# The down-projection of a hybrid encoder block by seven products of halved matrices, and forms remade product by product

## The chip, the core and the metric

The kernel runs on one core of one Trainium2 chip. The metric is the time of one execution in microseconds on that core. The engines are TensorE (PE, with PEld for its weight loads), VectorE (DVE), ScalarE (ACT), GpSimd (POOL) and the sync engine (SP), which here only issues DMAs. Matrices are float32; each is split into a high part in fp32r and the rest, and a product is three matmuls (high x high, high x low, low x high).

## The reference

One layer of a bidirectional encoder block, 2048 rows of width 1024: attention and a recurrent group, an output projection onto the residual (its result is called x1 in the kernel), then a gated MLP with a short convolution, and a final norm. The change lies in the last three lines:

```python
h = rms_norm(x, norm2_g[l])
u = depthwise_conv(h @ w_up[l], up_conv_w[l], up_conv_b[l], 1, 1)   # w_up: 1024 x 6144
gate, val = jnp.split(u, 2, axis=-1)
x = x + (jax.nn.gelu(gate) * val) @ w_down[l]                       # w_down: 3072 x 1024
return rms_norm(x, final_g)
```

## The kernel before

The attention, the recurrence and the output projection come first and are not touched. The MLP begins at about 1413 us of the span.

**Up-projection by steps.** The width of the gated product is cut into 24 tiles f of 128, the rows into two halves of 1024. Step i is one f for one half: steps 0 to 23 are f = 0 to 23 with the second half, steps 24 to 47 f = 23 to 0 with the first. The product of a step is a 2x2 product of halved matrices: on the weight's side a gate tile and a value tile, each in two halves of the inner width; on the side of the rows four blocks of 512 rows by 512. It is formed by seven products instead of eight, from sums of the halves. Such a sum, split into its high and low part, is called a form here. `a_forms` makes the seven forms of a step's weights (tiles `fa`) a step ahead: the sums on POOL (`a_srcs`, L1298 to L1306), the splits on ACT (L141) and DVE (L146). The forms of the rows (tiles `fb`, 7 products by 4 pieces of 128 of the inner width) stay over a half's 24 steps; there is one buffer for each.

`step` (from line 1530) issues seven products of 4 x 3 = 12 matmuls each (L1388). The products have four banks of PSUM: products 0 to 3 have banks 0 to 3, and products 4, 5 and 6 go on adding into banks 0, 3 and 2. So before product 5 (the sixth) TensorE waits until DVE has read bank 3 with the add behind product 4 (L1469, `y<-pu,y`). Behind each product the loop calls three generators in this order: `before`, which finishes the previous step (adds, convolution taps at L1503 and L1512, GELU at L1525, gate times value at L1527, store to `g_d`); `nxt`, a form of the next step's weights; and `side`, work that is spread over many steps. Each engine runs its instructions in the order in which they are issued. At a step's start `load_w(i + 2)` issues the loads of the weights of two steps later on SP. Of the three buffers `raw` the second is free only when a split of the current step has read it, so SP's queue stands until then.

**The change between halves.** Forms of the first half of the rows need sums of blocks. `sums_ahead`, the side work of steps 2 to 17, loads four blocks a unit, makes four sums in DVE (L1259, L1261, L1578, L1580) and stores them to `t_d`; there are four units. In step 23 the products are issued tile by tile of the inner width instead (`step_by_tile`, seven banks), and behind each piece its form is remade (`form`, through a ring of nine tiles `rg` that `load_ring` fills).

**Down-projection.** It runs over four blocks of 512 rows, 24 tiles f each, and for each f over 4 row tiles and two halves of the output width, three matmuls each (L1706), 2304 in all, that add up in eight banks over f. A tile f of `w_down` and of `g_d` is loaded and split some units ahead. At a block's end the rows of x1 are added, normed and stored (L1716 to L1730).

Of the kernel before, what the change touches and what calls it, by code (L numbers as in the profile page):

```python
# [20 lines left out]
D = 1024  # L21
KT = 8
# [61 lines left out]
def block_kernel(ctx, tc, x, g1, wqkv, wxy, qkg, rope, cw, cb, wg, bg, lam, w_out, g2,  # L84
# [22 lines left out]
    t_d = [dram.tile([128, 4, 512], F32, name=f"t_d{k}") for k in range(4)]  # L107
    g_d = [dram.tile([128, S], F32, name=f"g_d{f}") for f in range(FT)]
# [55 lines left out]
    with tc.manual_schedule():  # L164
# [1061 lines left out]
        steps = [(1, f) for f in range(FT)] + [(0, f) for f in range(FT - 1, -1, -1)]  # L1226
        raws, fa, fb, got = {}, {}, {}, {}
# [340 lines left out]
        def sums_ahead():  # L1568

            for k in range(4):  # L1570
                yield from load_b(0, k)
                for _ in range(10):
                    yield
                yield from b_sums(0, k, DVE)
                b11, b12, b21, b22 = got.pop((0, k))
                t3 = t3s.pop((0, k))
                yield
                DVE.tensor_tensor(out=b11, in0=t3, in1=b11, op=ALU.add)  # L1578
                yield
                DVE.tensor_tensor(out=b21, in0=b21, in1=b11, op=ALU.subtract)  # L1580
                for _ in range(3):
                    yield
                for n, t in enumerate((t3, b12, b11, b21)):
                    dma(out=t_d[k][:, n, :], in_=t)
                for _ in range(6):
                    yield

        ring, todo = [], []

        def load_ring():  # L1590
# [4 lines left out]
            k, j = n // 7, ORDER[n % 7]  # L1595
            t = tbp[n % 9 // 5].tile([128, 512], F32, tag=("t3", "b0", "b1", "b2", "b3", "b0", "b1", "b2", "b3")[n % 9],
                                     name="rg")
            src = {0: h2_d[0][:, k, :], 4: h2_d[0][:, k + 4, :], 5: h2_d[1][:, k + 4, :]}
            for m, jj in enumerate((2, 3, 1, 6)):
                src[jj] = t_d[k][:, m, :]  # L1600
            dma(out=t, in_=src[j])
            ring.append(t)

        def step_by_tile(i, before, made, change=False):

            for k in range(made, 4):
# [3 lines left out]
                for n, j in enumerate(by_tile(i, k)):  # L1610
# [5 lines left out]
                    if change:  # L1616
                        form(j, k, ring[7 * k + n])
                        load_ring()
            run(out)
            return conv(i)  # L1620

# [6 lines left out]
        side = sums_ahead()  # L1628
        for i in range(1, len(steps)):
            if i == FT - 2:  # L1630
                run(side)
                for _ in range(9):
                    load_ring()
            if i == FT - 1:
                left = chain(wait(2), step_by_tile(i, left, 0, True))
                run(load_w(i + 2))
                run(a_forms(i + 1))
            elif i < len(steps) - 1:
                left = step(i, left, side if i > 1 else iter(()), a_forms(i + 1))


        with ExitStack() as ph:
            pool = opener(ph)
            units = [(c, f) for c in range(NB - 1, -1, -1) for f in range(FT)]
            gw, x1s, po, rw = {}, {}, {}, {}
            HELD = 3

            def load(n):
                if n >= len(units) or n in rw:
                    return  # L1650
                c, f = units[n]
                if n == 0:
                    wraw = flat(rawp.tile([128, KT, 128], F32, tag="raw", name="wraw"))
                    graw = tbp[0].tile([128, 512], F32, tag="t3", name="graw")
                else:
                    wraw = wrp.tile([128, D], F32, tag="w", name="wraw")
                    graw = grp.tile([128, 512], F32, tag="g", name="graw")
                dma(out=wraw, in_=w_down[f])
                dma(out=graw, in_=g_d[f][:, c * 512:(c + 1) * 512])
                rw[n] = wraw, graw  # L1660

            def prep0():

                load(0)
                yield
                yield
                yield
                wraw, graw = rw[0]
                g = [tbp[0].tile([128, 512], F32R, tag=f"b{n}", name="dg") for n in (2, 3)]
                split(g[0], g[1], graw, ACT, DVE)  # L1670
                yield
                w_hi = flat(rawp.tile([128, KT, 128], F32R, tag="raw", name="dw"))
                w_lo = [tbp[0].tile([128, 512], F32R, tag=f"b{n}", name="dw") for n in (0, 1)]
                for j in range(2):
                    cols = slice(j * 512, (j + 1) * 512)
# [177 lines left out]
```

## Time and profile before

| | |
|---|---|
| median of 3 runs | 2924.38 us (2922.33 to 2928.16) |
| profiled execution | 2926.08 us, its span 2924.3 us |
| granted TensorE clock, mean | 0.986 |
| PE, PEld busy | 2811.0, 2236.7 us |
| DVE, ACT, POOL busy | 1989.4, 1508.5, 689.2 us |
| bytes moved by DMA | 329.42 MB |

A line of a group gives the source line, the engine, the operation, what it writes and reads, shapes and count, then busy time and mean ns of one, then idle time of the engine ahead of it and what ended it. In a timeline the first two numbers are start and length in us, and brackets give idle time ahead of the instruction. Matmuls overlap and their ends are modelled: their pace is read from starts, not from their lengths.

### The profile page before, as it was taken

To read this page: it belongs to the slowest core of one execution; us is meant where nothing else is said; L and a number is where in the kernel's file an instruction comes from. 1 tells how busy PE (TensorE), PEld (TensorE's weight loads), DVE (VectorE), ACT (ScalarE), POOL (GpSimd) and SP (SyncE) were. 2 spreads that over 40 slices of the span, in tenths; PEclk is the share of its full clock that TensorE was granted. 3 is DMA by queue.
4 is the path that set the end of the run, shared out by engine and by line. 5 is a ranking of instruction groups with operands and counts; after the bars stand their busy time and mean duration, and the time that the engine had idled before them with its cause. 6 is when DMAs were issued, how large, how long until landed. Compare 5 with 4: busy or idle time off the path is not lost.

```text
span 2924.3 us, 33492 instructions
## 1 busy us (share of the span) xinstructions
PE 2811.0 (96%) x12304; PEld 2236.7 (76%) x12304; DVE 1989.4 (68%) x2541; ACT 1508.5 (52%) x2195; POOL 689.2 (24%) x575
## 2 busy tenths in 40 slices
PE   8998998999999999998889999989999999999998
PEld 6666786777777777787668788868888878888887
DVE  6766676888888888666577777787777663424243
ACT  5777534777777777534444444454444443323232
POOL 5224443011111111010022222222222312222221
PEclk9999998999999999999999999999999999999999
DMA  3233343111121121477423332232222236446362
GB/s 131 99 125 120 91 162 98 46 48 46 51 53 44 48 53 41 158 241 239 144 80 115 116 113 91 102 128 87 87 80 75 84 121 212 171 170 207 118 229 84
DMA packets 160629, 329.42 MB, mean 113 GB/s; under 512 B 25488, under 2 KB 65296, under 8 KB 160336
## 3 DMA queue, kind: packets, MB, share of 16 engines
q1 hardware_dynamic: 151248, 293.73, 30.8%
q10 hardware_dynamic: 9216, 33.56, 2.9%
q8 instruction: 96, 1.57, 0.2%
q14 instruction: 69, 0.57, 0.1%
HBM read 230.29 MB, written 89.06 MB: 109 GB/s over the span
## 4 chain that ended last, share of the span: by engine, by line
PE 71%; DVE 7%; DMA 2%; ACT 1%; issue 1%; SPq 0%; POOL 0%; DVEq 0%; ACTq 0%; POOLq 0%
PE pu L1388 28%; PE po L1706 17%; PE po L1163 4%; PE mx L814 4%; PE s L974 4%; PE s L973 4%; PE b L1012 4%; PE b L1010 4%; PE a L1000 4%; DVE mxt L819 1%; DMA sc<-sig_d 1%; DVE u L1503 1%; DVE plo L990 1%; DVE fa L146 1%; DVE y L1469 1%
## 5 line engine op out<-in xcount | busy, mean ns | idle before, releaser
L1388 PE MATMUL pu<-fb,fa 128*128 128x512 f32 x4011 | 934.3, 394 | 27.0 <-DVE y L1469 14.5
L1388 PEld LDWEIGHTS pu<-fb,fa 128*128 128x128 f32 x4011 | 755.7, 189 | 203.7 <-DVE y L1469 17.1
L1706 PE MATMUL po<-dw,dg 128*128 128x512 f32 x2304 | 525.3, 390 | 3.7 <-DVE dw L146 2.0
L1706 PEld LDWEIGHTS po<-dw,dg 128*128 128x128 f32 x2304 | 433.3, 188 | 95.6 <-DVE dw L146 2.6
L819 DVE TENSOR_REDUCE mxt<-mx 128x2 f32<-128x1024 f32 x244 | 298.2, 1222 | 83.4 <-PE mx L814 83.1
L983 ACT ACTIVATE phi<-s 128x1024 fp32r<-128x1024 f32 x256 | 263.0, 1027 | 154.0 <-PE s L974 146.8
L146 DVE TENSOR_TENSOR dw<-wraw,dw 128x1024 fp32r<-128x1024 f32 (+1 forms) x97 | 148.5, 1532 | 282.2 <-ACT dw L141 278.2
L990 DVE TENSOR_TENSOR plo<-p,phi 128x1024 fp32r<-128x1024 f32 x256 | 330.7, 1292 | 7.8 <-ACT p L984 7.7
L984 ACT ACTIVATE p<-s 128x1024 f32<-128x1024 f32 x256 | 261.3, 1021 | 0.2 <-DVE plo L990 0.2
L1503 DVE SCALAR_TENSOR_TENSOR u<-y,ucw_s,u 128x1024 f32<-128x1024 f32 (+1 forms) x192 | 248.8, 1296 | 3.1 <-ACT u L1512 1.4
L146 POOL TENSOR_TENSOR dg<-graw,dg 128x512 fp32r<-128x512 f32 x95 | 130.5, 1374 | 404.3 <-ACT dg L141 404.3
L1298 POOL TENSOR_TENSOR s<-raw 128x512 f32<-128x512 f32 x46 | 61.5, 1337 | 677.2 <-DMA raw<-in_w_up 635.3
L146 DVE TENSOR_TENSOR fa<-raw,fa 128x512 fp32r<-128x512 f32 (+1 forms) x188 | 149.9, 798 | 86.6 <-ACT fa L141 86.6
L973 PE MATMUL s<-qa,ka 128*128 128x512 f32 x512 | 203.3, 397 | 3.8 <-ACT p L984 2.2
L974 PE MATMUL s<-qb,kb 65*128 65x512 f32 x512 | 203.5, 398 | 0.0
L141 ACT ACTIVATE dg<-graw 128x512 fp32r<-128x512 f32 x96 | 60.4, 629 | 258.4 <-issue 200.5
L814 PE MATMUL mx<-ka,qa 128*128 128x512 f32 x512 | 168.3, 410 | 11.6 <-DVE mxt L819 4.5
L1512 ACT ACTIVATE u<-y,ucb_s,ucw_s 128x1024 f32<-128x1024 f32 (+1 forms) x96 | 119.2, 1242 | 104.7 <-DVE y L1469 103.8
L1163 PE MATMUL po<-wo_hi,m 128*128 128x512 f32 x512 | 167.4, 403 | 4.6 <-ACT fb L1028 3.7
L814 PEld LDWEIGHTS mx<-ka,qa 128*128 128x128 f32 x512 | 139.5, 310 | 40.0 <-DVE mxt L819 8.6
L1469 DVE TENSOR_TENSOR y<-pu,u 128x512 f32<-128x512 f32 x144 | 99.2, 690 | 92.0 <-PE pu L1388 91.8
L1012 PE MATMUL b<-phi,ones_r 128*65 128x512 f32 x512 | 161.2, 396 | 0.0
(252 smaller groups left out, 4359.1 us busy)
## 6 DMA issues: line engine op xcount, KB each, us to landing
wraw<-in_w_down SPq DMA_DIRECT2D x96, 512.0 KB
raw<-in_w_up SPq DMA_DIRECT2D x94, 512.0 KB
graw<-g_d SPq DMA_DIRECT2D x96, 256.0 KB
x_t<-in_x SPq DMA_DIRECT2D x44, 512.0 KB
l<-lru_d SPq DMA_DIRECT2D x32, 512.0 KB
g_d<-u ACTq DMA_DIRECT2D x24, 512.5 KB
g_d<-u ACTq DMA_DIRECT2D x24, 511.5 KB
q_d<-t SPq DMA_DIRECT2D x16, 512.0 KB
```

The costliest lines, as they stand in the source:

```text
L146: e_lo.tensor_tensor(out=lo, in0=src, in1=f32(hi), op=ALU.subtract)
L814: PE.matmul(ps, lhsT=qa[u].rearrange("p (q t) -> p t q", t=4)[:, qt], rhs=ka[group(u)][:, kc * 512:(kc + 1) * 512], start=True, stop=True)
L819: DVE.tensor_reduce(out=mxt[u % 2][:, qt, 2 * kp:2 * kp + 2], in_=pair, axis=AX.X, op=ALU.max)
L973: PE.matmul(ps[:, h], lhsT=ka[g][:, keys], rhs=qa[u], start=True, stop=False)
L974: PE.matmul(ps[:, h], lhsT=kb[g][:, keys], rhs=qb[u], start=False, stop=True)
L983: ACT.activation(out=p_hi, in_=ps, func=AF.Exp)
L990: DVE.tensor_tensor(out=p_lo, in0=p, in1=f32(p_hi), op=ALU.subtract)
L1012: PE.matmul(pb[u], lhsT=ones_r[:, 0:65], rhs=p_hi[:, h], start=False, stop=i == 7 and h == 1)
L1163: PE.matmul(ps[i], lhsT=lh[:, rows], rhs=rh[:, k, i * 512:(i + 1) * 512], start=n == 0, stop=n == 23)
L1388: PE.matmul(ps, lhsT=lh, rhs=rh, start=start and n == 0, stop=stop and n == 2, skip_group_check=more)
L1503: DVE.scalar_tensor_tensor(out=u[:, 0:w], in0=y[:, o:o + w], scalar=ucw_s[:, t * FT + f, o:o + 1], in1=u[:, 0:w], op0=ALU.mult, op1=ALU.add)
L1706: PE.matmul(po[r][j], lhsT=g(a, rows), rhs=w(b, j), start=f == 0 and m == 0, stop=f == FT - 1 and m == 2)
```

## The change

The down-projection becomes 24 further steps, 48 to 71, of the same kind as a step of the up-projection. The width of the gated product is cut into three blocks q of eight tiles f (order 2, 1, 0), the rows into eight pairs rp of 128-row tiles. One side is `g_d`, halved in f and in rows; the other is `w_down`, halved in f and in the output width. A step is again 7 products of 12 matmuls at the same line, so 24 x 84 = 2016 matmuls. The forms of `w_down` take the place of the forms of the rows and are remade three times, before steps 48, 56 and 64.

- `sums_ahead` is now a unit of 14 calls, two steps, for any four sources. Besides the 4 units of rows there are 12 of `w_down`, stored to `wt_d`: nine units run in steps 2 to 19, seven in steps 24 to 37.
- `remake` takes the place of the step by tiles: in steps 23, 47, 55 and 63 it remakes four forms behind each product. Nine source tiles are loaded a step ahead, the other 19 as the ring comes free.
- Each down step loads 2 x 4 pieces of `g_d` (128 x 2 x 128) as its weights and adds its result to four tiles of the residual, loaded a step ahead (`load_acc`) and, for q = 2 and 1, stored back to DRAM on ACT's queue. For q = 0 the rows are normed, scaled and stored to the output. 

The vector engine in a step with a unit of sums, before; lines 1259, 1261, 1578 and 1580 are the unit's, `y_12709<-pu,y_12709` is the add that reads bank 3:

```order
L146 TENSOR_TENSOR fa<-raw,fa 128x512
L1259 TENSOR_TENSOR t_13260<-b 128x512
L1503 SCALAR_TENSOR_TENSOR u_12711<-y_12709,ucw_s,u_12711 128x1024 x2
L146 TENSOR_TENSOR fa<-s,fa 128x512
L1261 TENSOR_TENSOR b<-b 128x512
L1469 TENSOR_TENSOR u_12712<-pu,u_12712 128x512
L1503 SCALAR_TENSOR_TENSOR u_12710<-y_12708,ucw_s,u_12710 128x1024
L146 TENSOR_TENSOR fa<-raw,fa 128x512
L1503 SCALAR_TENSOR_TENSOR u_12710<-y_12708,ucw_s,u_12710 128x1024
L1469 TENSOR_TENSOR y_12709<-pu,u_12712 128x512
L146 TENSOR_TENSOR fa<-s,fa 128x512
L1578 TENSOR_TENSOR b<-t_13260,b 128x512
```

The add of bank 3 follows this row, and the unit's fourth operation comes behind it. Now, with lines 1596 to 1602 as the unit's:

```order
L1596 TENSOR_TENSOR t_18189<-b 128x512
...
L1598 TENSOR_TENSOR b<-b 128x512
L1485 TENSOR_TENSOR u_12724<-pu,u_12724 128x512
L1519 SCALAR_TENSOR_TENSOR u_12722<-y_12720,ucw_s,u_12722 128x1025
L147 TENSOR_TENSOR fa<-raw,fa 128x512
L1600 TENSOR_TENSOR b<-t_18189,b 128x512
L1519 SCALAR_TENSOR_TENSOR u_12722<-y_12720,ucw_s,u_12722 128x1025
L1485 TENSOR_TENSOR y_12721<-pu,u_12724 128x512
L147 TENSOR_TENSOR fa<-s,fa 128x512
L1602 TENSOR_TENSOR b<-b 128x512
L1485 TENSOR_TENSOR y_12721<-pu,y_12721 128x512
```

All four operations of a unit stand ahead of the add of bank 3, the last row, in each of the sixteen units.

The vector engine in step 55, a change step of the down stage, up to the add that reads bank 3 (the last row, `x_t<-pu,x_t`); `fb<-rg` are the remade forms:

```order
L147 TENSOR_TENSOR fb<-rg,fb 128x512 x4
L147 TENSOR_TENSOR fa<-s,fa 128x512
L147 TENSOR_TENSOR fb<-rg,fb 128x512 x4
L1485 TENSOR_TENSOR u_20934<-pu,u_20934 128x512
L147 TENSOR_TENSOR fa<-raw,fa 128x512
L147 TENSOR_TENSOR fb<-rg,fb 128x512 x4
L1485 TENSOR_TENSOR x_t<-pu,x_t 128x512
L1708 TENSOR_TENSOR x_t<-x_t,u_20934 128x512
L147 TENSOR_TENSOR fa<-s,fa 128x512
L147 TENSOR_TENSOR fb<-rg,fb 128x512 x4
L1485 TENSOR_TENSOR x_t<-pu,x_t 128x512
```

Sixteen forms stand ahead of the gating add; before, no forms were made in the steps of `step` at all.

The sync engine at the change into the down stage, rows of steps 46 and 47 with the middle left out:

```order
L90 DMA rg<-wt_d_108 128x512
L90 DMA rg<-wt_d_105 128x512
L90 DMA raw<-g_d_125 128x2x128
...
L90 DMA raw<-g_d_132 128x2x128
L90 DMA rg<-wt_d_106 128x512
L90 DMA rg<-wt_d_107 128x512
L90 DMA rg<-wt_d_108 128x512
```

After nine source tiles come the 16 loads of the weights of two steps, and only behind them the tenth source tile.

The diff, cut to its core (the old down-projection and the old `sums_ahead` are left out):

```diff
+        steps += [(q, rp) for q in (2, 1, 0) for rp in range(NV)]
+        UP = 2 * FT
...
+            if i >= UP:
+                q, rp = steps[i]
+                for e in range(2):
+                    raw = rawp.tile([128, KT, 128], F32, tag="raw", name="raw")
+                    raws[i].append(flat(raw))
+                    for k in range(4):
+                        dma(out=raw.rearrange("p (r k) c -> p r k c", r=2)[:, :, k, :],
+                            in_=g_d[8 * q + 4 * e + k][:, rp * 256:rp * 256 + 256].rearrange("p (r c) -> p r c", r=2))
+                    yield
+                return
...
+            if i >= UP:
+                a12, a21 = a21, a12
...
+        def sums_ahead(srcs, d, n):
+            b = []
+            for m, src in enumerate(srcs):
+                t = tbp[0].tile([128, 512], F32, tag=f"b{m}", name="b")
+                dma(out=t, in_=src)
+                b.append(t)
+            yield
+            for _ in range(n):
+                yield
+            b11, b12, b21, b22 = b
+            t3 = tbp[0].tile([128, 512], F32, tag="t3", name="t3")
+            DVE.tensor_tensor(out=t3, in0=b22, in1=b12, op=ALU.subtract)
+            yield
+            DVE.tensor_tensor(out=b12, in0=b12, in1=b11, op=ALU.subtract)
+            yield
+            DVE.tensor_tensor(out=b11, in0=t3, in1=b11, op=ALU.add)
+            yield
+            DVE.tensor_tensor(out=b21, in0=b21, in1=b11, op=ALU.subtract)
+            yield
+            yield
+            for m, t in enumerate((t3, b12, b11, b21)):
+                dma(out=d[:, m, :], in_=t)
+            yield
+            yield
...
+        def remake(what):
+            for n in range(28):
+                form(n // 4, n % 4, ring[n])
+                load_ring(*what)
+                if n % 4 == 3:
+                    yield
+            ring.clear()
...
+        sums_w = [sums_ahead(down_srcs(n), wt_d[n], 6) for n in (8, 9, 10, 11, 4, 5, 6, 7, 0, 1, 2, 3)]
+        side = chain(*[sums_ahead(rows_srcs(k), t_d[k], 6) for k in range(4)], *sums_w[:5])
+        changes = {FT - 1: rows_, UP - 1: downs[2], UP + NV - 1: downs[1], UP + 2 * NV - 1: downs[0]}
...
+        def down(i, before, side, nxt):
+            run(load_w(i + 2))
...
+            for j in range(7):
+                own = {4: 0, 5: 3, 6: 2}.get(j, j)
+                ps = b[j] = bank(own) if own == j else b[own]
+                for k in range(4):
+                    mms(i, j, k, ps, own == j and k == 0, own == j and k == 3, own != j)
+                if j == 1:
+                    copy(u, b[0])
+                if j == 2:
+                    add(u, u, b[1])
+                next(before, None)
+                if j == 3:
+                    add(x22, x22, b[2])
+                    DVE.tensor_tensor(out=x21, in0=x21, in1=u, op=ALU.add)
+                if j == 4:
+                    add(x22, x22, b[3])
+                    DVE.tensor_tensor(out=x12, in0=x12, in1=u, op=ALU.add)
+                if j == 5:
+                    add(x11, x11, b[0])
+                    DVE.tensor_tensor(out=x22, in0=x22, in1=u, op=ALU.add)
+                    load_acc(i + 1)
+                if j == 6:
+                    add(x12, x12, b[3])
+                next(nxt, None)
+                next(side, None)
...
         for i in range(1, len(steps)):
-            if i == FT - 2:
+            if i + 1 in changes:
                 run(side)
                 for _ in range(9):
-                    load_ring()
+                    load_ring(*changes[i + 1])
+            what = remake(changes[i]) if i in changes else side
+            nxt = a_forms(i + 1)
+            if i < UP:
+                left = step(i, left, what if i > 1 else iter(()), nxt)
+            else:
...
+                left = down(i, left, what, nxt)
+            run(nxt)
+            if i in changes:
+                run(what)
             if i == FT - 1:
-                left = chain(wait(2), step_by_tile(i, left, 0, True))
-                run(load_w(i + 2))
-                run(a_forms(i + 1))
...
+                side = chain(*sums_w[5:])
```

More of the change, by code (lines that the diff above doesn't have):

```diff
@@ new lines, in block_kernel, with row_tile, load_acc @@
+        acc, dpool = {}, []
+        gf_s = []
+        def row_tile(i, r):
+            n = 2 * steps[i][1] + r
+            return x1_d[n // 4][n % 4], n * 128
+        def load_acc(i):
+            if i < UP or i >= len(steps):
+                return
+            acc[i] = []
+            for r in range(2):
+                for c in range(2):
+                    m = 2 * r + c
+                    if dpool:
+                        t = dpool[0].tile([128, 512], F32, tag=f"x{m}", name="x1_t")
+                    else:
+                        t = tbp[i - UP].tile([128, 512], F32, tag=f"b{m}", name="x1_t")
+                    dma(out=t, in_=row_tile(i, r)[0][:, c * 512:c * 512 + 512])
+                    acc[i].append(t)
@@ new lines, in down, with rest @@
+        def down(i, before, side, nxt):
+            run(load_w(i + 2))
+            b = {}
+            x11, x12, x21, x22 = acc.pop(i)
+            u = (dpool[0] if dpool else tbp[0]).tile([128, 512], F32, tag="u" if dpool else "t3", name="u2")
+            for j in range(7):
[22 more added lines that the diff above has]
+                next(side, None)
+            run(before)
+            def rest():
+                add(x21, x21, b[2])
+                x = ((x11, x12), (x21, x22))
+                if steps[i][0]:
+                    yield
+                    yield
+                    for r in range(2):
+                        for c in range(2):
+                            dma(out=row_tile(i, r)[0][:, c * 512:c * 512 + 512], in_=x[r][c], eng=ACT)
+                    yield
+                    return
+                ys = []
+                for r in range(2):
+                    s2 = dpool[1].tile([128, 2], F32, tag="s2", name="s2")
+                    for c in range(2):
+                        junk = tbp[1].tile([128, D], BF16, tag="b0", name="junk")
+                        ACT.activation(out=junk[:, 0:512], in_=x[r][c], func=AF.Square, accum_out=s2[:, c:c + 1])
+                    y = dpool[1].tile([128, 1], F32, tag="r1", name="r1")
+                    DVE.tensor_tensor(out=s2[:, 0:1], in0=s2[:, 0:1], in1=s2[:, 1:2], op=ALU.add)
+                    ACT.activation(out=y, in_=s2[:, 0:1], func=AF.Sqrt, scale=1.0 / D, bias=eps_s)
+                    ys.append(y)
+                yield
+                for r in range(2):
+                    DVE.reciprocal(out=ys[r], in_=ys[r])
+                    for c in range(2):
+                        DVE.scalar_tensor_tensor(out=x[r][c], in0=x[r][c], scalar=ys[r], in1=gf_s[c],
+                                                 op0=ALU.mult, op1=ALU.mult)
+                    yield
+                    n0 = row_tile(i, r)[1]
+                    for c in range(2):
+                        dma(out=out[n0:n0 + 128, c * 512:c * 512 + 512], in_=x[r][c], eng=ACT)
+                yield
+            return rest()
@@ new lines, in block_kernel @@
+                    load_ring(*changes[i + 1])
[3 more added lines that the diff above has]
+                left = step(i, left, what if i > 1 else iter(()), nxt)
+            else:
+                if i == UP + 2 * NV:
+                    for c in range(2):
+                        t = tbp[1].tile([128, 512], F32, tag=f"b{2 + c}", name="gf_s")
+                        dma(out=t, in_=gf[:, c * 512:c * 512 + 512].to_broadcast([128, 512]))
+                        gf_s.append(t)
+                left = down(i, left, what, nxt)
```

196 lines of the change are left out of this document (26 added, 170 removed).

## The prediction

> **What bounds the kernel now.** I read the page's groups first, then the busy time by stretches, then the timeline of single steps. Two groups of matmuls fill the second half of the span:
>
> ```profile
> L1388 PE MATMUL pu<-fb,fa 128*128 128x512 f32 x4011 | 934.3, 394 | 27.0 <-DVE y L1469 14.5
> L1706 PE MATMUL po<-dw,dg 128*128 128x512 f32 x2304 | 525.3, 390 | 3.7 <-DVE dw L146 2.0
> ```
>
> The last column is idle time before the group: TensorE waits 27 us in 900 us of up-projection and 4 us in the down-projection. The stretches agree (stretch, its length, then PE, PEld, DVE, ACT and POOL busy with counts, the granted clock, DMA share, GB/s):
>
> ```profile
> 2100.00:2200.00 100.00, 100.00 (x436) 81.54 (x436) 72.04 (x89) 46.00 (x77) 28.16 (x21) 1.00 0.23 79
> 2500.00:2600.00 100.00, 100.00 (x443) 82.81 (x442) 37.58 (x33) 35.13 (x49) 24.88 (x18) 1.00 0.51 180
> ```
>
> TensorE is full at full clock, so time falls only by matmuls that are not issued or waits that go. A step of the up-projection is seven products of 12 matmuls. Its length is the distance between one row of consecutive steps, the copy that follows a step's first product (start, length, engine; in brackets idle time before):
>
> ```profile
> 2312.77 0.60 ACT L1472 ACTIVATE u<-pu 128x512 f32<-128x512 f32 x1 [0.21 <-PE pu L1388]
> 2321.13 0.68 DVE L1469 TENSOR_TENSOR y<-pu,y 128x512 f32<-128x512 f32 x1
> 2321.73 0.68 DVE L146 TENSOR_TENSOR fa<-raw,fa 128x512 fp32r<-128x512 f32 x1
> 2325.90 1.29 POOL L1298 TENSOR_TENSOR s<-raw 128x512 f32<-128x512 f32 x1 [13.70 <-DMA raw<-in_w_up]
> 2332.09 0.60 ACT L1472 ACTIVATE u<-pu 128x512 f32<-128x512 f32 x1 [0.20 <-PE pu L1388]
> ```
>
> 2332.09 - 2312.77 = 19.32 us a step, 2.76 a product. The first product ended at 2312.56, so the sixth starts at 2312.56 + 4 x 2.76 = 2323.60. It adds into bank 3, which the vector engine's add at 2321.13 must first have read; that ends at 2321.81. **1.8 us of slack** stand there, and whatever is put ahead of this add eats them. The same place decides most of what follows.
>
> **The products.** The old down-projection runs from the first to the last of these rows:
>
> ```profile
> 2388.13 6.34 PE L1706 MATMUL po<-dw,dg 128*128 128x512 f32 x25 [0.88 <-DVE y L1469]
> 2899.70 16.48 PE L1706 MATMUL po<-dw,dg 128*128 128x512 f32 x72
> ```
>
> 2899.70 + 16.48 - 2388.13 = 528.0 us for 2304 matmuls. Now there are 24 steps of 84, 2016. They are issued by the same function as the up-projection, over tiles of the same pools, so I take 19.32 a step: 463.7, **-64.4 us**. The other bound is the old down-projection's pace, 100 us / 443 = 0.226 x 84 = 18.96, another 8.6 less. In an ordinary down step the vector engine has 7 splits, 6 reads of PSUM and 3 additions, 0.6 us each by the two starts at 2321.13 and 2321.73: 9.6 against some 13.9 in an up step (72 of 100 us, five steps), with no convolution; it adds no wait.
>
> **The sums ahead.** Sixteen units (4 of rows, 12 of weights) take four vector operations each, where four did. A unit lasts 14 calls, two steps exactly, so its four operations always fall behind products 0, 1, 2 and 3, all ahead of the add that gates the sixth product. Before, a unit's operations drifted, and where three stood ahead it went so:
>
> ```profile
> 1521.99 1.78 DVE L1259 TENSOR_TENSOR t<-b 128x512 f32<-128x512 f32 x1
> 1526.80 0.69 DVE L1261 TENSOR_TENSOR b<-b 128x512 f32<-128x512 f32 x1
> 1532.20 0.68 DVE L1578 TENSOR_TENSOR b<-t,b 128x512 f32<-128x512 f32 x1
> 1532.80 0.68 DVE L1469 TENSOR_TENSOR y<-pu,y 128x512 f32<-128x512 f32 x1
> 1533.54 2.81 PE L1388 MATMUL pu<-fb,fa 128*128 128x512 f32 x11 [1.04 <-DVE y L1469]
> 1612.23 288.12 PE L1388 MATMUL pu<-fb,fa 128*128 128x512 f32 x1250 [1.14 <-DVE y L1469]
> ```
>
> TensorE waited 1.04 and 1.14 us, twice in four units: 2.2 us. Slack is less when POOL's sums start late (their weights come behind the units' transfers):
>
> ```profile
> 1635.84 1.29 POOL L1298 TENSOR_TENSOR s<-raw 128x512 f32<-128x512 f32 x1 [12.99 <-DMA raw<-in_w_up]
> 1640.15 0.60 ACT L1472 ACTIVATE u<-pu 128x512 f32<-128x512 f32 x1 [0.17 <-PE pu L1388]
> 1649.39 0.68 DVE L1469 TENSOR_TENSOR y<-pu,y 128x512 f32<-128x512 f32 x1
> ```
>
> Here the sixth product starts at 1639.98 + 11.04 = 1651.02 and the add ends at 1650.07: 0.95 of slack, with POOL starting 1.4 us before the step instead of 3.2. With every other step a unit's, I take this slack: 4 x 0.6 - 0.95 = 1.45 a unit, 16 x 1.45 = 23.2, less the 2.2 there already: **+21.0**. Bounds: 0.6 a unit with the full slack (+7.4), 2.0 with POOL later still (+29.8).
>
> **The change in the middle.** Today forms are remade tile by tile while TensorE runs a step by tiles:
>
> ```profile
> 1902.25 4.28 ACT L141 ACTIVATE fb<-rg 128x512 fp32r<-128x512 f32 x8 [1.79 <-PE pu L1388]
> 1902.92 5.52 DVE L146 TENSOR_TENSOR fb<-rg,fb 128x512 fp32r<-128x512 f32 x9 [0.53 <-ACT fb L141]
> 1914.55 4.60 PE L1388 MATMUL pu<-fb,fa 128*128 128x512 f32 x12 [6.49 <-ACT y L1472]
> 1920.48 2.57 PE L1388 MATMUL pu<-fb,fa 128*128 128x512 f32 x10 [1.32 <-DVE u L1469]
> 1924.28 9.02 PE L1388 MATMUL pu<-fb,fa 128*128 128x512 f32 x38 [1.23 <-DVE fb L146]
> 1936.45 19.58 PE L1388 MATMUL pu<-fb,fa 128*128 128x512 f32 x84 [3.15 <-DVE y L1469]
> 1956.43 3.95 PE L1388 MATMUL pu<-fb,fa 128*128 128x512 f32 x16 [0.40 <-DVE y L1469]
> ```
>
> The waits are 12.6 us, and 12 matmuls took 4.60 instead of 2.9: 14.3 lost. A form costs the vector engine 5.52 / 9 = 0.6. Remade product by product, forms j stand behind product j, so 16 forms stand ahead of the gating add. Its time, from the step's start: product 0 ends at 2.8, 0.6 for ScalarE's half, 16 forms 9.6, four taps 5.0, three adds 1.8: 19.8, where the sixth product wanted 13.8. Taps are from this row:
>
> ```profile
> 2313.21 2.61 DVE L1503 SCALAR_TENSOR_TENSOR u<-y,ucw_s,u 128x1025 f32<-128x1025 f32 x2
> ```
>
> 6.0 of waiting. After such waits the clock is halved for a while; the stretches show 0.53 and 0.55:
>
> ```profile
> 1471.44 61.06 PE L1388 MATMUL pu<-fb,fa 128*128 128x512 f32 x252 [8.80 <-DVE y L1469]
> 1471.40:1478.00 6.60, 6.56 (x16) 5.22 (x17) 3.50 (x5) 3.98 (x5) 2.49 (x2) 0.53 0.25 79
> 1914.50:1918.30 3.80, 3.75 (x10) 2.98 (x11) 2.27 (x4) 2.59 (x5) 0.00 (x0) 0.55 0.90 287
> ```
>
> 16 matmuls in 6.6 us instead of 3.7 after 8.8 idle; 1.7 lost after 6.5 (their mean, 2.3, is taken for the long waits below). So 6.0 + 1.7 = 7.7 replace 14.3: **-6.6**. The rest of the forms is ready in time, since the next step needs them a product at a time. (The Trainium skill, TensorE: Matmul & The Clock Gate, section The HAM clock gate, says the array falls to half rate after an idle window of about 3.4 us and returns after one busy window; by that each long wait would cost 1.7, the sum would be 1.8 us lower, and 6.6 us at half rate above say it can last longer.)
>
> **Three new changes** (steps 47, 55, 63). Here the sync engine's queue matters too:
>
> ```profile
> SPq L90 <- DVE fa L146: 197.1, 21, 13.5
> ```
>
> This is the view of waits over ten steps: in each, twice, the queue stands until a split frees the weight buffer. In a change step the loads of form sources 9 to 27 are queued behind that wait. In down steps and step 47 the split is that of product 2, so source 9, needed right behind it, isn't even issued. From a split's end to the use of a 512 KB weight took 2325.90 - 2322.41 = 3.5 us. Issues take this long on the sync engine and on ScalarE:
>
> ```profile
> 2341.80 0.33 SPq L90 DMA_DIRECT2D raw<-in_w_up  x1
> 2304.61 0.33 ACTq L90 DMA_DIRECT2D g_d<-u  x1
> ```
>
> Four more are issued ahead of source 9 than ahead of a weight, 4 x 0.33 = 1.3, and 256 KB more have to land: 5.0 us of standstill for ACT and DVE. Between nothing (source 9 comes in time) and 8 (all nine next sources land first, 2.3 MB at the 287 GB/s of the stretch above) this is nearest to the row. Step 47: 19.8 + three splits 1.8 + 5.0 - 13.8 = 12.8, and 2.3 for the clock: 15.1. Steps 55 and 63 have no taps but one more add, and four stores issued on ACT, of which 1.0 shows: 2.8 + 0.6 + 9.6 + 1.8 + 2.4 + 1.0 + 5.0 - 13.8 = 9.4, and 2.3: 11.7 each. Together **+38.5**; 17 with no standstill and a warm clock. Rows of x that are added up come a step ahead and cost nothing; without that cover, some 4 us a step.
>
> **The end.** The last matmul ended at 2916.18, the span is 2924.3, and the last scaling stood here:
>
> ```profile
> 2916.26 0.63 ACT L1718 ACTIVATE junk<-x_t 128x512 bf16<-128x512 f32 x1 [1.92 <-DVE x_t L1716]
> 2917.89 0.29 ACT L1724 ACTIVATE r<-s,eps_s 128x1 f32<-128x1 f32 x1 [0.23 <-DVE s L1720]
> 2919.36 1.41 DVE L1730 SCALAR_TENSOR_TENSOR x_t<-x_t,r,gf_s 128x512 f32<-128x512 f32 x2
> ```
>
> It ended 4.6 after the last matmul. Now two row tiles end together: an add 0.7, a root 0.3, two squares 1.6 with their reads, small steps 0.6, four scalings 2.8: 6.0, **+1.4**.
>
> **The sum**: -64.4 + 21.0 - 6.6 + 38.5 + 1.4 = -10.1. The profiled execution took 2926.1, 1.7 above the median, so 2916.0 for it and 2914.3 at the median: I say **2915**.
>
> **Rivals.** *Changes well hidden*: the form sources come in time and the gating add is late only by the vector engine's own work. For it: nine sources are loaded a step ahead. Against it: the queue order. Each of three changes gives back 5.0 and about 1 of clock, -18: 2897; with sums at 0.6, 2883. *Slower: the weights' transfer falls behind the sums' traffic.* Each unit puts 1 MB of loads and 1 MB of stores behind the weight on the sync queue. POOL started 3.2 us ahead of its step without, 1.4 with such traffic, and slack fell from 1.8 to 0.95. From 0.5 us after the step's start on, no slack is left in any of these 32 steps; each us more then costs 0.5 to 0.8 in both steps of a unit: 16 x (1.2 + 0.3) = +24, 2938. Against it: the old down-projection moved 180 GB/s beside a full TensorE, more than these steps will. *No gain per step*: the four loads of 512-byte pieces and the rows of x through DRAM delay the next step's weights, some 0.5 us a step, 2927, no change; the transfers' share of 0.51 in the old down-projection speaks against it.
>
> **Chances.** The forecast 0.55, hidden changes 0.20, slower 0.17, no gain per step 0.08. The range 2893 to 2938 leaves out the far ends of the two rivals, some 0.2. A measurement of this kernel tells 0.2% (5.8 us) from nothing, so faster is below 2918.5, only 3.5 above my number: of the forecast's 0.55 I count 0.35 faster, 0.17 the same and 0.03 slower. With the rivals: faster 0.55, same 0.25, slower 0.20.
>
> **What would show it.** Steps of 19.32 us between copies in the down stage; TensorE waiting about 1.5 us on the add of bank 3 in every second up step of the units; one long wait, on that add, in each change step: about 6, 13, 9 and 9 us, and form sources as the releaser of ACT there. Wrong if the change steps wait on something else, if the unit steps don't wait, or if down steps are longer than 19.4.

## The result and the profile after

The changed kernel takes 2947.53 us (median of 4 runs, 2942.63 to 2949.98) where the kernel before took 2925.55 on the same chip: ratio 1.007, 95% interval 1.0057 to 1.0082. The forecast was 2915. The profiled execution is the lowest of the four, 2942.63, with a span of 2940.8. Different executions reach the MLP some us apart, so profiles are compared from its first product on. Its row in the kernel before, and in the changed one:

```profile
1413.16 5.06 PE L1388 MATMUL pu<-fb,ax 128*128 128x512 f32 x21 [0.88 <-DVE x_t L1169]
```

```profile
1410.11 5.01 PE L1404 MATMUL pu<-fb,ax 128*128 128x512 f32 x21 [0.87 <-DVE x_t L1170]
```

2924.30 - 1413.16 = 1511.1 us before, 2940.84 - 1410.11 = 1530.7 after: 19.6 more, where the forecast had 10.1 less.

TensorE's group on the page has all the matmuls of both projections now; the view of waits from 1480 us on (engine and what it waited for, us in total, times, longest) says what TensorE stood for:

```profile
L1404 PE MATMUL pu<-fb,fa 128*128 128x512 f32 x6027 | 1412.5, 396 | 95.7 <-DVE y L1485 62.8
PE pu L1404 <- DVE y L1485: 55.2, 18, 20.2
PE pu L1404 <- DVE x_t L1485: 29.5, 3, 14.6
```

95.7 us of idle time, against 27.0 + 3.7 in the two groups before, and all but 11 of it in 21 waits on the add that reads a bank of PSUM. The timeline of TensorE shows some of them: two units of sums, the change in the middle, the last unit, the three new changes, and one more wait in step 48, behind the first of these (1.76).

```profile
1512.14 38.92 PE L1404 MATMUL pu<-fb,fa 128*128 128x512 f32 x168 [1.79 <-DVE y L1485]
1552.69 38.92 PE L1404 MATMUL pu<-fb,fa 128*128 128x512 f32 x168 [1.62 <-DVE y L1485]
...
1923.17 40.97 PE L1404 MATMUL pu<-fb,fa 128*128 128x512 f32 x168 [6.13 <-DVE y L1485]
...
2210.99 193.47 PE L1404 MATMUL pu<-fb,fa 128*128 128x512 f32 x840 [1.35 <-DVE y L1485]
2424.61 21.83 PE L1404 MATMUL pu<-fb,fa 128*128 128x512 f32 x84 [20.15 <-DVE y L1485]
2448.19 135.52 PE L1404 MATMUL pu<-fb,fa 128*128 128x512 f32 x588 [1.76 <-DVE x_t L1485]
2598.30 157.23 PE L1404 MATMUL pu<-fb,fa 128*128 128x512 f32 x672 [14.59 <-DVE x_t L1485]
2768.68 162.90 PE L1404 MATMUL pu<-fb,fa 128*128 128x512 f32 x696 [13.15 <-DVE x_t L1485]
```

168 matmuls are two steps, a unit: every unit waits once, every change once, at the add that the forecast named. Between them only step 48 waits. A down step's length is the distance of its copies (this source line from 2490 to 2560 us: count, duration, first and last start):

```profile
L1488 ACT ACTIVATE u<-pu x4: 599/599/599, 2495.4 to 2553.4; 128x512 f32<-128x512 f32 x4
```

(2553.4 - 2495.4) / 3 = 19.33 us. So places and pace were right, and the waits are longer than forecast. The account below takes 19.32 from the distance of each step's first matmul to the next step's, and puts the rest to what stands in the step:

| term | forecast | from the trace |
|---|---|---|
| products | -64.4 | -65.2 |
| sums ahead | +21.0 | +32.5 |
| change in the middle | -6.6 | -6.9 |
| three new changes | +38.5 | 24.7 + 17.3 + 16.0 = +58.0 |
| end | +1.4 | +1.1 |

That makes +19.5, and the profiles differ by 19.6. The products gain 0.8 more than forecast because TensorE also stood 0.88 ahead of the first row of the old down-projection. The rows above give the third term too: from 2210.99 to 2768.68 + 162.90 = 2931.58 there are 2880 matmuls, at 0.23 each 662.4 us, so 58.2 are lost there. (By the distances of the copies the last change comes to 17.7 and the three to 59.7, which one expectation below uses. But 1.75 of that is only ScalarE's copy in step 64 coming late, and TensorE does not wait there.)

**Inside a change.** Step 47 on the vector engine, then on ScalarE, on the sync engine's queue and on POOL:

```profile
2394.39 3.59 DVE L147 TENSOR_TENSOR fb<-rg,fb 128x512 fp32r<-128x512 f32 x4
...
2401.02 2.49 DVE L147 TENSOR_TENSOR fb<-rg,fb 128x512 fp32r<-128x512 f32 x4
...
2405.22 0.68 DVE L147 TENSOR_TENSOR fa<-raw,fa 128x512 fp32r<-128x512 f32 x1
2405.82 0.68 DVE L147 TENSOR_TENSOR fb<-rg,fb 128x512 fp32r<-128x512 f32 x1
2412.53 1.38 DVE L147 TENSOR_TENSOR fb<-rg,fb 128x512 fp32r<-128x512 f32 x2 [6.03 <-ACT fb L142]
2415.23 0.69 DVE L147 TENSOR_TENSOR fb<-rg,fb 128x512 fp32r<-128x512 f32 x1 [1.32 <-ACT fb L142]
...
2418.24 5.71 DVE L147 TENSOR_TENSOR fb<-rg,fb 128x512 fp32r<-128x512 f32 x4
2423.87 0.68 DVE L1485 TENSOR_TENSOR y<-pu,y 128x512 f32<-128x512 f32 x1
2411.87 1.32 ACT L142 ACTIVATE fb<-rg 128x512 fp32r<-128x512 f32 x2 [11.04 <-DMA rg<-wt_d]
2407.87 3.98 SPq L90 DMA_DIRECT2D rg<-wt_d  x7
2434.43 1.94 SPq L90 DMA_DIRECT2D raw<-g_d  x4
2418.40 1.65 POOL L1314 TENSOR_TENSOR s<-raw 128x512 f32<-128x512 f32 x1 [22.78 <-DMA rg<-in_w_down]
```

The split of product 2 ends at 2405.90 and frees the weight's buffer. Four loads of 512-byte pieces are issued (1.94 / 4 = 0.48 us each, where I took 0.33), so the tenth form source is issued at 2407.87 and used at 2411.87. The vector engine stands for 6.03 us and, since the sources behind it land one by one, for 1.32 more. Then the weights have landed too, POOL starts its sums of them (the row names another DMA, but the operation reads `raw`), and the next four forms take 5.71 us where four took 2.49. Behind these stands the gating add. The first four forms of the step, at 2394.39, take 3.59, and the split ahead of them 1.19 where 0.68 is usual, beside the last of POOL's earlier sums. Step 55 is the same: 7.12 and 1.23 of standstill, then four forms in 5.71; in step 63 it is 6.84 and 0.47, then 5.70.

Is it POOL that stretches the forms? From 1500 us on (count, then shortest, median and longest in ns), for the forms and for additions that read PSUM:

```profile
L147 DVE TENSOR_TENSOR fb<-rg,fb x112: 674/682/1781, 1905.9 to 2779.9; 128x512 fp32r<-128x512 f32 x112
L1485 DVE TENSOR_TENSOR y<-pu,u x135: 680/693/695, 1509.6 to 2435.7; 128x512 f32<-128x512 f32 x135
```

Of the 112 forms 86 ran while POOL was idle, and none of these took over 0.69 us; of the 26 beside an operation of POOL 11 took longer, up to 1.78. Of the 135 additions 45 ran beside POOL, and none was longer. So here the operations with both inputs in SBUF are stretched, and only beside POOL.

The clock around the wait, the first stretch from its end on, the second around all of it (length, PE busy with count, then the other engines and the clock):

```profile
2424.60:2432.00 7.40, 7.39 (x22) 5.87 (x23) 7.40 (x12) 3.99 (x7) 2.56 (x1) 0.67 0.67 225
2409.00:2429.50 20.50, 4.89 (x12) 3.83 (x13) 15.65 (x19) 11.37 (x19) 4.98 (x4) 0.50 0.72 240
```

22 matmuls take 7.4 us, at 0.23 they take 5.1: 2.3 lost here. At half clock the core spent 20.5 us, some 15 of them idle.

### The profile page after: what moved, and what is told of

Read it like the earlier page. It is cut to its first block, busy times and chain, and to the rows that moved or that the text cites. A ratio compares the mean times of both kernels' runs of the same rounds, so it can differ in the third digit from the quotient of the medians.

```text
span 2940.8 us, 34037 instructions
## 1 busy us (share of the span) xinstructions
PE 2761.9 (94%) x12016; PEld 2185.9 (74%) x12016; DVE 2225.2 (76%) x2954; ACT 1524.1 (52%) x2308; POOL 710.5 (24%) x576
## 4 chain that ended last, share of the span: by engine, by line
PE 54%; DVE 16%; DMA 6%; issue 4%; ACT 2%; SPq 1%; ACTq 0%; POOL 0%; DVEq 0%; POOLq 0%
PE pu L1404 31%; DVE u L1519 4%; PE mx L815 4%; PE s L975 4%; PE s L974 4%; PE b L1013 4%; PE b L1011 4%; PE a L1001 4%; DVE fa L147 2%; DMA b<-in_w_down 2%; PE po L1164 2%; DVE y L1485 2%; DVE fb L147 1%; SPq L90 1%; DMA l<-lru_d 1%
## 5 line engine op out<-in xcount | busy, mean ns | idle before, releaser
L1404 PE MATMUL pu<-fb,fa 128*128 128x512 f32 x6027 | 1412.5, 396 | 95.7 <-DVE y L1485 62.8
L1404 PEld LDWEIGHTS pu<-fb,fa 128*128 128x128 f32 x6027 | 1139.2, 190 | 366.9 <-DVE y L1485 73.0
L1314 POOL TENSOR_TENSOR s<-raw 128x512 f32<-128x512 f32 x70 | 97.9, 1399 | 1038.8 <-DMA raw<-in_w_up 677.3
L147 DVE TENSOR_TENSOR fa<-raw,fa 128x512 fp32r<-128x512 f32 (+1 forms) x284 | 244.3, 860 | 100.7 <-ACT fa L142 99.7
L1519 DVE SCALAR_TENSOR_TENSOR u<-y,ucw_s,u 128x1024 f32<-128x1024 f32 (+1 forms) x192 | 264.5, 1378 | 1.7
L142 ACT ACTIVATE fa<-raw 128x512 fp32r<-128x512 f32 (+1 forms) x284 | 175.9, 620 | 171.3 <-PE pu L1404 90.1
L147 DVE TENSOR_TENSOR fa<-s,fa 128x512 fp32r<-128x512 f32 (+1 forms) x213 | 157.9, 741 | 43.0 <-ACT fa L142 43.0
L1541 ACT ACTIVATE u<-u 128x1024 f32<-128x1024 f32 (+1 forms) x48 | 51.0, 1062 | 255.2 <-DVE u L1519 255.2
L142 ACT ACTIVATE fa<-s 128x512 fp32r<-128x512 f32 (+1 forms) x213 | 132.5, 622 | 57.0 <-PE pu L1404 31.9
L1001 PE MATMUL a<-phi,vt 128*128 128x512 f32 x512 | 160.6, 395 | 0.0
```

Source lines behind the costliest of these rows:

```text
L142: ACT.activation(out=hi, in_=src, func=AF.Copy)
L147: e_lo.tensor_tensor(out=lo, in0=src, in1=f32(hi), op=ALU.subtract)
L1001: PE.matmul(pa[u], lhsT=vt[:, kt, group(u), 0:128], rhs=p_hi[:, h], start=kt == 0, stop=kt == 15)
L1404: PE.matmul(ps, lhsT=lh, rhs=rh, start=start and n == 0, stop=stop and n == 2, skip_group_check=more)
L1519: DVE.scalar_tensor_tensor(out=u[:, 0:w], in0=y[:, o:o + w], scalar=ucw_s[:, t * FT + f, o:o + 1], in1=u[:, 0:w], op0=ALU.mult, op1=ALU.add)
```

## The experiments

Theory A, in most runs, is that the time is the forecast's sum with two terms too small: the units' waits (operations ahead of the gate) and the three changes (sources late by the queue, then work of POOL and of the vector engine at the same time). Theory B is the rival named in each expectation, mostly waits that only move. "Against the changed kernel" is the difference of the two ratios to the kernel before times 2925.5 us; its interval is about 5 to 8 us on either side.

**Sums four calls later.** Three of a unit's four operations then stand behind the gating add, and one ahead of the next step's.

```diff
-        side = chain(*[sums_ahead(rows_srcs(k), t_d[k], 6) for k in range(4)], *sums_w[:5])
+        side = chain(wait(4), *[sums_ahead(rows_srcs(k), t_d[k], 6) for k in range(4)], *sums_w[:5])
...
-                side = chain(*sums_w[5:])
+                side = chain(wait(4), *sums_w[5:])
```

> The only edit: four empty calls ahead of each chain of sums, so that a unit's four vector operations come behind products 4, 5, 6 and 0 instead of 0 to 3. Theory A (the units cost time because their operations stand ahead of the add that reads bank 3): the sixteen waits of 1.5 to 3.1 us in the up steps, 31 us together, go; one operation of 0.6 us still stands ahead of the add and fits into the slack; about -28 to -31 us against the changed kernel, 2916 to 2920. Theory B (the units cost time by their transfers or because the vector engine has too much to do, wherever its operations stand): the waits only move to another place and the time falls by less than 10 us.

2912.39 us, ratio 0.9961 (0.9948 to 0.9974): 32 us less than the changed kernel. TensorE in the units:

```profile
1604.44 38.99 PE L1404 MATMUL pu<-fb,fa 128*128 128x512 f32 x168 [0.30 <-DVE y L1485]
1643.73 38.90 PE L1404 MATMUL pu<-fb,fa 128*128 128x512 f32 x168 [0.30 <-DVE y L1485]
```

The sixteen waits are all but gone, for the same operations and the same traffic: where they stand was nearly the whole price, theory A.

**Sums one call later**, to see the law of that price: `wait(1)` instead of `wait(4)` leaves three operations ahead of the gate.

> The sums start one call later instead of four, so that three of a unit's four operations stand ahead of the gating add instead of four, and the first no longer stands in the first call. Theory A (each operation ahead of the add costs its own 0.6 us): the sixteen waits fall from 1.96 to 1.36 us on average, 10 us in all, 2937. Theory B (the first operation collides with POOL's sums at the step's start and lasts 1.8 us instead of 0.6, or delays the convolution's finish): they fall by about 1.7 to 0.3 us, some 25 us in all, 2922.

Ratio 1.0027 (1.0014 to 1.0039), 2929.26 us: 13 less than the changed kernel. The distance of two rows of a unit, 1555.70 - 1516.08 = 39.62, is 1.0 more than two steps; the sixteen waits (distances of starts, less 0.23 for the matmul itself) are 1.26 us on average, and 1.96 with four operations.

```profile
1516.08 38.91 PE L1404 MATMUL pu<-fb,fa 128*128 128x512 f32 x168 [0.79 <-DVE y L1485]
1555.70 38.93 PE L1404 MATMUL pu<-fb,fa 128*128 128x512 f32 x168 [0.71 <-DVE y L1485]
```

Theory A's step of 0.6 an operation (0.70 measured), not B's collapse. With n operations ahead, 0.6 n - 0.5 gives 1.9 and 1.3 for four and three. For one it gives 0.1, and the run with late sums has 0.31 on average: its one operation falls beside POOL's sums and takes 1.78 us in most units, so there it costs more than its 0.6.

**Form sources ahead of the second weight tile.** In steps 47, 55 and 63 the second tile of the weights is loaded behind product 4, so the form sources no longer queue behind it (the edit in `step`; `down` has the same).

```diff
-            run(load_w(i + 2))
+            w = load_w(i + 2)
+            if i in changes and i >= UP - 1:
+                next(w)
+            else:
+                run(w)
...
+                if slot == 4:
+                    run(w)
```

> The only edit: in steps 47, 55 and 63 the second weight tile is loaded behind product 4 and no longer at the step's start, so that nothing stands on the sync queue ahead of the loads of form sources 9 to 27. Theory A (ACT and DVE stand still because these loads are queued behind the wait for the weight buffer): the standstill of 6 to 7 us at the tenth source goes in each of the three steps, the waits of 20.2, 14.6 and some 13 us fall to about 11 to 13, 7 and 7, together -15 to -22 us against the changed kernel. Theory B (the ring's transfers themselves are too slow, 19 tiles of 256 KB in one step): the standstill is spread over the later sources and the time falls by 5 us or less.

2917.68 us, ratio 0.9982 (0.9972 to 0.9991): 26 less than the changed kernel. TensorE's waits at the changes:

```profile
2418.41 21.62 PE L1404 MATMUL pu<-fb,fa 128*128 128x512 f32 x84 [9.72 <-DVE y L1485]
2443.66 136.95 PE L1404 MATMUL pu<-fb,fa 128*128 128x512 f32 x588 [3.62 <-DVE x_t L1485]
2586.19 156.64 PE L1404 MATMUL pu<-fb,fa 128*128 128x512 f32 x672 [5.59 <-DVE x_t L1485]
2748.30 151.90 PE L1404 MATMUL pu<-fb,fa 128*128 128x512 f32 x648 [5.47 <-DVE x_t L1485]
```

20.15 became 9.72, 14.59 became 5.59, 13.15 became 5.47; 1.9 came back in the step behind the first, whose weights are later now. The queue held 8 to 10 us a change, standstill and collision together, not 5.0.

**Both edits.**

> The sums start four calls later and, in steps 47, 55 and 63, the second weight tile is loaded behind product 4. Theory A: the two dear parts are separate places (unit operations ahead of the gating add; form sources queued behind the weight's load), so their gains of 35 and 30 us add up: 2947.5 - 65 = 2882, between 2876 and 2888. Theory B: they share the vector engine's lag, so that one gain is partly the other's: 2895 to 2902, as all three changes together gave 2901.7. Under A the shortfall of all three together is then the price of the own banks, about 20 us, against 6 when they were changed alone.

2889.87 us, ratio 0.989 (0.9868 to 0.9912): 53 less than the changed kernel, where the single gains are 32 + 26 = 58, and the fastest here with all of the work in it. The times alone don't decide: by the ratio it is 2893 on the scale of 2925.5, with an interval from 2887 to 2900, which touches A's range (up to 2888) and B's (from 2895). The trace is for A, since each edit leaves here the waits that it left alone (the changes 9.50 and 4.37, 5.03, 5.51; the units 0.5 by starts at most). What is left of step 47 is the vector engine itself, which stands for no moment from 2365.5 to behind the gating add at 2384.19. In step 48, the last row, its taps run beside POOL's sums:

```profile
2376.98 2.49 DVE L147 TENSOR_TENSOR fb<-rg,fb 128x512 fp32r<-128x512 f32 x4
2379.39 1.28 DVE L1519 SCALAR_TENSOR_TENSOR u<-y,ucw_s,u 128x1025 f32<-128x1025 f32 x1
...
2381.78 2.49 DVE L147 TENSOR_TENSOR fb<-rg,fb 128x512 fp32r<-128x512 f32 x4
2384.19 0.68 DVE L1485 TENSOR_TENSOR y<-pu,y 128x512 f32<-128x512 f32 x1
...
2399.12 4.55 DVE L1519 SCALAR_TENSOR_TENSOR u<-y,ucw_s,u 128x1025 f32<-128x1025 f32 x2
```

**Own banks for products 4, 5 and 6 of a change**, so that no product of it waits for a read (the results are added up on the vector engine).

```diff
-                own = {4: 0, 5: 3, 6: 2}.get(j, j)
+                free = i in changes
+                own = j if free else {4: 0, 5: 3, 6: 2}.get(j, j)
...
+                    if free:
+                        add(g2c, u2, b[3])
```

> The only edit: in the four change steps products 4, 5 and 6 have banks of their own (three more adds in DVE), so that the sixth product waits for no add; the sync queue is as in the changed kernel. Theory A (the long waits come from the gate on bank 3, while the forms are needed only later, a product at a time): the four waits of 6, 20, 15 and 13 us go; since the tenth source is still late, smaller waits stay where the next step wants forms or banks, up to 8 us each; -30 to -45 us against the changed kernel. Theory B (the vector engine's 28 forms in a step are the bound, whatever the banks): TensorE waits in the next step for forms instead, and the time falls by less than 12 us.

2953.6 us, ratio 1.0109 (1.0092 to 1.0126): 11 more than the changed kernel. The wait moved a step on and split up, as theory B had it:

```profile
2430.58 13.93 PE L1404 MATMUL pu<-fb,fa 128*128 128x512 f32 x48 [13.25 <-ACT y L1488]
2448.41 5.30 PE L1404 MATMUL pu<-fb,fa 128*128 128x512 f32 x12 [3.90 <-ACT u L1488]
2457.77 151.97 PE L1404 MATMUL pu<-fb,fa 128*128 128x512 f32 x648 [4.07 <-DVE x_t L1485]
```

13.25 + 3.90 + 4.07 = 21.2, where 20.15 + 1.76 = 21.9 stood, with three more additions and more pieces at half clock. The gate was only where the lag of the engines behind it showed.

**All three edits.**

> All three edits together. Theory A: the gains add up to what the waits held, 31 of units and 55 to 60 of changes with the halved clock behind them, less what the extra adds cost: -75 to -90 us against the changed kernel, 2857 to 2872, faster than the kernel before by about 2%. Theory B: -20 us or less, about the time before.

2901.72 us, ratio 0.9925 (0.991 to 0.994). Short of the expectation by 30 us: it counted on a gain from the own banks, and beside the two good edits they cost (0.9925 - 0.989) x 2925.5 = 10 us, as they did alone.

**Forms spread behind the gate.** On the version with both edits, one or two forms (two or three in the last two changes) stand behind each of products 0 to 3, the others behind products 4 to 6 and in the next step.

```diff
+        PACE = {FT - 1: ((2, 2, 1, 1, 6, 6, 4), (3, 3)), UP - 1: ((1, 1, 1, 1, 7, 7, 5), (6,)),
+                UP + NV - 1: ((3, 2, 2, 2, 4, 4, 3), (3, 3, 3)), UP + 2 * NV - 1: ((3, 2, 2, 2, 4, 4, 3), (3, 3, 3))}
...
-            what = remake(changes[i]) if i in changes else side
+            if i in changes:
+                g = remake(changes[i])
+                what = paced(g, PACE[i][0])
```

> On the version with late sums and second weight tile behind product 4, the forms of a change are no longer made four behind each product: one or two behind products 0 to 3 (two or three in the last two changes), the others behind products 4 to 6 and in the step that follows, product by product. Theory A (a change's wait is the forms that stand ahead of the gating add): few stand there now, and the waits fall from 6.6, 14, 6 and 6 us to about 2 each, with less time at half clock: 20 us under the version it is built on, about 2862. Theory B (the vector engine's work over the two steps of a change, about 47 us where two steps last 38.6, sets the time wherever the forms stand): the waits move behind the gate and into the next step, and at most 8 us are won, about 2874 or more.

2891.45 us, ratio 0.9894 (0.9868 to 0.9919): nothing won. Around step 47 TensorE now stands three times:

```profile
2383.90 12.88 PE L1404 MATMUL pu<-fb,fa 128*128 128x512 f32 x48 [2.63 <-DVE y L1485]
2404.02 10.44 PE L1404 MATMUL pu<-fb,fa 128*128 128x512 f32 x36 [7.24 <-DVE y L1485]
2418.74 6.49 PE L1404 MATMUL pu<-fb,fa 128*128 128x512 f32 x21 [4.27 <-DVE x_t L1485]
```

14.1 us, and 9.50 + 4.37 = 13.9 without the spreading: theory B. With the queue out of the way, the vector engine's work over two steps sets the time there, wherever the forms stand.

**A fourth of the forms' low parts on POOL**, on the version with both edits, and on the spread one.

```diff
-            split(t[:, 0], t[:, 1], src, ACT, DVE)
+            split(t[:, 0], t[:, 1], src, ACT, POOL if k == 3 and ring else DVE)
```

> On the version with late sums and second weight tile behind product 4, the low part of every fourth form of a change is made by POOL instead of the vector engine: seven of 28. Theory A (what is left of a change's wait is vector work: in that version the vector engine stands for no moment from 2369 to 2396 around step 47, with 16 forms ahead of the gating add): four forms fewer stand ahead of it, 2.4 us less in each of four changes and less time at half clock, 10 us in all, ratio to before 0.9855. Theory B (POOL's sums of the next weights are queued behind its new work, or it slows the vector engine as it does where both run): no gain or a loss, ratio 0.989 or more.

> The same on the version with the forms spread behind the gate and into the next step, which itself won nothing (0.9894). Theory A (there the vector engine's work over two steps sets the time): 7 x 0.6 = 4.2 us less in each change, 12 to 17 us in all, ratio about 0.984 to 0.986. Theory B: a weight that arrives late, not the vector engine, sets the next step's start there: ratio 0.989 or more.

Ratios 0.9905 (0.989 to 0.992) and 0.9943 (0.9924 to 0.9961): no gain on the first, a loss on the second. In the first of them, on POOL and on the vector engine:

```profile
2364.64 1.29 POOL L1316 TENSOR_TENSOR s<-s,raw 128x512 f32<-128x512 f32 x1
2371.71 2.28 POOL L147 TENSOR_TENSOR fb<-rg,fb 128x512 fp32r<-128x512 f32 x1
2383.94 1.71 POOL L1322 TENSOR_TENSOR s<-raw,s 128x512 f32<-128x512 f32 x1
2384.45 2.95 DVE L147 TENSOR_TENSOR fb<-rg,fb 128x512 fp32r<-128x512 f32 x3
2389.01 1.88 DVE L147 TENSOR_TENSOR fb<-rg,fb 128x512 fp32r<-128x512 f32 x3
```

A low part takes 1.3 to 2.3 us on POOL, and three forms of the vector engine beside POOL's work 2.95 instead of 1.88. POOL's sums of the next weights wait their turn behind them too: of four that otherwise follow one another, the second stands at 2364.64 and the fourth at 2383.94. Work given to POOL comes back as slower work on the vector engine.

**No new changes.** The forms of `w_down` are left out at steps 47, 55 and 63; the forms of the rows are multiplied in the down stage in their place.

```diff
-        changes = {FT - 1: rows_, UP - 1: downs[2], UP + NV - 1: downs[1], UP + 2 * NV - 1: downs[0]}
+        changes = {FT - 1: rows_}
```

> The forms of w_down are left out in steps 47, 55 and 63 (the forms of the rows stay in their place and are multiplied in the down stage); the sums and everything else are as in the changed kernel. Theory A: what the three steps lose, 24.7 + 17.3 + 17.7 = 59.7 us by the distances of their copies, is the price of remaking, and goes altogether: 2888, between 2884 and 2892. Theory B: part of it belongs to the passage into the down stage itself (loads of 512-byte pieces, accumulator rows, stores) and stays: 5 to 10 us at step 47 and 2 to 3 at the others, 2898 to 2903.

2885.22 us, ratio 0.9874 (0.9852 to 0.9896): 57 less than the changed kernel, where the starts of the matmuls gave 58.0. Theory A: the price is the remaking's own, and the passage into the down stage costs nothing:

```profile
2250.32 624.02 PE L1404 MATMUL pu<-fb,fa 128*128 128x512 f32 x2712 [0.17 <-DVE y L1485]
```

**The products alone**: this edit and the late sums.

> Late sums, and the forms of w_down left out at steps 47, 55 and 63 (the forms of the rows are multiplied in the down stage in their place). What is left of the change are the products, the change in the middle and the end: -64.4 - 6.6 + 1.4 by the forecast, of which the 2.2 of waits that sums cost before go too: -71.8, ratio 0.9755. Theory B (gains of single parts do not add up, since waits move): ratio over 0.98.

2855.98 us, ratio 0.9762 (0.9746 to 0.9778), 69.6 less than before, where the forecast's terms make 71.8. From the change in the middle on the view shows no wait:

```profile
1907.24 937.60 PE L1404 MATMUL pu<-fb,fa 128*128 128x512 f32 x4056 [6.45 <-DVE y L1485]
```

-69.6 for this, 32 for the units, 57 for the three changes: +19.4, and the changed kernel's ratio says +20.5. The parts add up.

## Why the prediction was wrong

**Right: the products, the middle and the end.** A down step takes 19.33 us for 19.32. The products alone gave -69.6 us, with the forecast's -71.8 inside the interval. In the middle one wait of 6.13 stands where 6.0 was said. The end took 2940.8 - 2931.6 = 9.2 after the last matmul, 8.1 before.

**Right: the places.** The waits stand at the add that reads bank 3: sixteen in the units, one in each change, with form sources as ScalarE's releaser in the new ones. One more, in step 48, was not forecast. The rival without gain per step is refuted by the steps' length. The rival with well hidden changes is refuted by 7 to 8 us of standstill. The slower rival came from the wrong place: it wanted all 32 steps of the units to wait, and half of them have no wait; what it said of the sums' traffic, that POOL starts later, holds in part (below).

**Wrong: the term "three new changes", +38.5, measured +58.0, and in it the 5.0 us of standstill.** This step failed, and it alone turns the sign: with 58.0 in its place the sum is +9.4. In step 47, on the forecast's own scheme, the sixth product comes 20.3 us late (20.15, and 0.16 by which a matmul's modelled length passes its pace). That is made of 8.1 for the vector engine's own work, where 7.8 was put; of 7.35 of standstill, where 5.0 was put; of 5.71 - 2.49 = 3.2 for four forms that ran beside POOL's sums, where nothing was put; and of 1.6 for the first split and forms of the step, (1.19 - 0.68) + (3.59 - 2.49), stretched in the same way, where nothing was put either. Another 1.9 stood in the next step, and the clock took 24.7 - 20.3 - 1.9 = 2.5 where 2.3 was put (17.3 - 14.75 = 2.5 and 16.0 - 13.3 = 2.7 in the other two). The run with both edits agrees: without the queue step 47 waits 9.50 + 0.16 = 9.7, which is 8.1 + 1.6. The upper bound of 8 in the text held for the standstill but for step 55's 8.35; it did not hold what the late weights set off. The run with the sources ahead of the weights shows the queue as the cause, and the counts of stretched operations show POOL's work as the cause of the rest.

The price of that collision lay in a row quoted in the prediction: the operation at 1521.99 took 1.78 us where the same kind took 0.69. I counted every such operation at 0.6. The Trainium skill (GPSIMD Engine Reference, section 1, Specifications) says that GpSimd shares its SBUF interfaces with VectorE, and contends with vector instructions that have two SBUF inputs; every form's low part is one, and the rows above agree, with 5.71 us for 2.49.

**Wrong in size: "sums ahead", +21.0, measured +32.5.** The law was right, 0.6 an operation ahead of the gate less the slack, and the runs with four and three operations there fit 0.6 n - 0.5. The slack of 0.95 was taken from a step ahead of which POOL had started 1.4 us early. With units back to back POOL started only 0.9 us before the step in this unit (the step's start is 1512.14 + 2 x 2.76 + 19.32 = 1537.0), and 0.95 in the median of the sixteen:

```profile
1536.06 1.28 POOL L1314 TENSOR_TENSOR s<-raw 128x512 f32<-128x512 f32 x1 [13.46 <-DMA raw<-in_w_up]
1540.53 1.79 DVE L1596 TENSOR_TENSOR t<-b 128x512 f32<-128x512 f32 x1
1551.95 0.68 DVE L1485 TENSOR_TENSOR y<-pu,y 128x512 f32<-128x512 f32 x1
```

The wait mostly goes with this lead: 1.51 in the unit with a lead of 1.39, as the forecast has it; 2.37 with 0.38; 3.10 where POOL started 0.56 after the step. On average 1.96 a unit instead of 1.45 is 8 us over sixteen; it is the bound of 2.0 that the text had, "with POOL later still". The other 3 us are 1.4 at half clock, once, behind a wait of 2.38, and 0.1 to 0.2 a unit beside the gate, less 0.9 that the waits before had cost beyond the 2.2 counted. With this miss alone the sum would have been -10.1 + 11.5 = +1.4, no change.

**The range** added up terms at their likely values and opened its upper end for one rival; both mis-sized terms went up together, since both are lateness of the same engine at the same gate.

## What to carry to other kernels

Work spread behind products is free only up to the slack of the next gate: count what stands ahead of it, and move it behind, before counting what it costs in all; four calls' delay was worth 1.1% here. Where a queue stands on a buffer, everything issued behind it is late by the whole wait, the issue of what is ahead, and whatever starts when it all lands at once; put the loads with the nearest use first. When removing a gate or spreading work moves a wait and leaves its sum, the engine behind it is full. Here neither other banks, nor spreading, nor giving work to POOL won anything then; leaving the forms out did.

## What was not expected of the hardware

Vector operations on two SBUF tensors take up to 2.7 times as long while POOL runs operations too: four forms 5.71 us for 2.49, one subtraction 1.79 for 0.68, two taps 4.55 for 2.60. Additions that read PSUM keep their 0.69. POOL's own rows grow from 1.3 to 2.3. Loads issued one right behind another take about 0.48 us each on the sync engine (four in 1.94), where a lone one took 0.33. After a wait of 20 us TensorE needed 7.4 us for 22 matmuls; the three long waits cost 2.5, 2.5 and 2.7 us more than their length, as worked out above.
